# Weight sums of the down projection started during gate and up, and row scale and offset spread over its units

## Chip, cores and metric

One NeuronCore of one Trainium2 chip runs the whole program. The metric is the device time of one execution in microseconds, the median over the runs shown. All times below are of the kernel before the change.

## What is computed

The reference is a decoder trunk of two layers over 512 positions of width 1024, in float32:

```python
for l in range(DEPTH):                                   # DEPTH = 2
    proj = x @ w_in[l]
    ...
    mix = jnp.concatenate([o_a, o_b], axis=-1) @ w_out[l]
    x = layer_norm(ALPHA * x + mix, ln1_g[l], ln1_b[l])
    ffn = (jax.nn.silu(x @ w_ffn_gate[l]) * (x @ w_ffn_up[l])) @ w_ffn_down[l]
    x = layer_norm(ALPHA * x + ffn, ln2_g[l], ln2_b[l])
```

`o_a` is a gated linear recurrence and `o_b` sparse attention with three branches; the change does not edit them. D_FF is 2816, that is 22 blocks of 128 columns for each of gate and up, and 22 blocks of rows for the down projection. `layer_norm` subtracts the mean, divides by the deviation, multiplies by `g` and adds `b`.

## The kernel before

**Products.** Each float32 product is made of three matmuls (`mm3`, lines 80 to 86): an operand is split into a rounded part (`whi`, `hop`, `xh`, `th`), made by a cast on ACT, and the remainder (`wlo`, ...), made by a subtraction on DVE; the product is hi x hi, hi x lo and lo x hi.

**Gate and up.** `seven` (line 126) works through 20 units to a layer, gate and up in turn, each two blocks of 128 weight columns against the 512 positions in halves of 256. A unit makes seven products in place of eight, in Strassen's manner, so it needs sums of weight blocks. `stage` (lines 94 to 108) loads a unit's weights: SP issues the loads of `s1`, `s3`, the big `a` (128x1024) and `d`; POOL issues DMAs that add a second block into `s1` and `s3` (lines 104 and 105). DVE makes two more sums in `a` (lines 153 and 162). `split` (line 110) casts on ACT (line 116) and subtracts on DVE (line 117) into a ring of six places. Each unit finishes two of its products inside the next unit. A table of `hooks` lets other work be called at the head of a unit.

**Scale and offset of the rows.** The residual rows are four tiles of 128x1024. `norm_rest` (lines 751 to 759), called by the hook of unit 3, loads the parameters of the first norm (line 704, on POOL's queue) and issues for each tile one multiplication (line 756) and one addition (line 757) on DVE.

**Down projection.** It starts at line 1010. For four groups q, of two blocks of rows each, it again makes seven products of 2x2 blocks. The weight sums are made by DMAs: S1(q) = wd[1,2q] + wd[1,2q+1] is loaded by SP and added to by POOL in `raw_w` (lines 1034 to 1039; the load is line 1036, the add line 1038), S1(3) in a place of its own, `ws` (lines 1060 and 1061). `first` (line 1053) multiplies with S1 into the PSUM tiles Y and then has POOL add wd[0,2q] to it (line 1074); `third` (line 1081) multiplies with that sum into E and has POOL add wd[0,2q+1] (line 1087); `fourth` (line 1089) multiplies with the result into Z. `second` (line 1076) multiplies with the plain p11(q) into M. The list at lines 1092 to 1094 gives the order in which these are called, up to fourth(2). In the loop that follows, `raw_w` makes S3(q) = wd[0,2q] + wd[1,2q] in the same three places as the S1 sums (tag `f`), and loads p12 and p22; fourth(3) stands inside its first turn. The weights are split by `split` (lines 1016 to 1019) into three places for `whi` and three for `wlo`. In the trace Y is `ps_s`, E `ps_d`, Z `ps_t`, and M is `ps_h` and `ps_o`.

**Order.** Each engine works its instructions in order, and so do the DMA queues of SP and POOL: a DMA that waits holds those behind it. The order comes from a scheduler that goes by priorities (`high_priority`, with the offsets in the code) and by when it thinks operands and places come free. A tag with `bufs` is a set of places that tiles take in turn, and a tile waits until the last reader of its place is done.

Of the kernel before, what the change touches and what calls it, by code (L numbers as in the profile page):

```python
# [34 lines left out]
class Kern:  # L35
# [58 lines left out]
    def stage(self, sa, sb):  # L94

        nc = self.nc
        with self.tc.high_priority(offset=3000):
            self.turn += 1
            tag, bufs = ("wr", 2) if self.turn % 3 else ("pt", 2) if self.turn == 3 else ("f", 3)
            a = self.sb.tile([128, 1024], F32, name="wraw", tag=tag, bufs=bufs)  # L100
            s1, s3, d = (self.sb.tile([128, 512], F32, name=n, tag=t, bufs=2) for n, t in (("ws1", "st"), ("ws3", "pc"), ("wd", "wd")))
            nc.sync.dma_start(s1, sb[:, 512:])
            nc.sync.dma_start(s3, sa[:, :512])
            nc.gpsimd.dma_start(s1, sb[:, :512], accum_op=OP.add)
            nc.gpsimd.dma_start(s3, sb[:, :512], accum_op=OP.add)
            nc.sync.dma_start(a, sa)
            nc.sync.dma_start(d, sb[:, 512:])
        return a, s1, s3, d
# [17 lines left out]
    def seven(self, units, R, hooks):  # L126
# [13 lines left out]
        for n, unit in enumerate(units + [None]):  # L140
# [8 lines left out]
            if unit:  # L149
                self.prod(D, s1, R["T1"], True)  # L150
                y = copy("sy", D)
                with self.tc.high_priority(offset=3000):
                    nc.vector.tensor_tensor(a[:, :512], s1, a[:, :512], op=OP.add)
                self.prod(B, a[:, 512:], R["R21"], True)
                unit[2]("11", B, x)
# [606 lines left out]
    def layer(self, l):  # L762
# [242 lines left out]

        self.seven([(io[w][l, j], io[w][l, j + 1], f(j)) for j in range(2, NF, 2) for w, f in (("wg", gate), ("wu", up))], R,
                   {3: lambda: self.norm_rest(l, 0, rows, None)})

        QS = 4
# [4 lines left out]
        def split(dst, src):  # L1016
            with tc.high_priority(offset=3000):
                nc.scalar.copy(dst[0], src)  # L1018
                nc.vector.tensor_tensor(dst[1], src, dst[0].bitcast(F32), op=OP.subtract)  # L1019

        def places(k):
# [11 lines left out]

        def raw_w(src, plus=None, tag=("wr", 2)):
            t = self.sb.tile([128, 1024], F32, name="wraw", tag=tag[0], bufs=tag[1])
            nc.sync.dma_start(t, src)
            if plus is not None:
                nc.gpsimd.dma_start(t, plus, accum_op=OP.add)
            return t

        def dprod(acc, w, r, start, stop):
# [8 lines left out]
        half = [[(H[2 * q + e][:, :, b * 256:(b + 1) * 256]) for e in range(2) for b in range(2)] for q in range(QS)]  # L1050
        sums, ops = {}, {}

        def first(q):

            with tc.high_priority(offset=3000):
                if q < 3:
                    s = raw_w(wd[1, 2 * q], wd[1, 2 * q + 1], ("f", 3))
                else:
                    s = self.big("ws").rearrange("p a b -> p (a b)")[:, :1024]
                    nc.sync.dma_start(s, wd[1, 2 * q])  # L1060
                    nc.gpsimd.dma_start(s, wd[1, 2 * q + 1], accum_op=OP.add)
            r11, r12, _, r22 = half[q]
# [6 lines left out]
            with tc.high_priority(offset=3000):  # L1069
                nc.vector.scalar_tensor_tensor(r11, t1, -1.0, r22, op0=OP.mult, op1=OP.subtract)  # L1070
            sums[q] = s
            dprod(Y, split_w(s), o1, q == 0, q == QS - 1)
            with tc.high_priority(offset=3000):
                nc.gpsimd.dma_start(s, wd[0, 2 * q], accum_op=OP.add)

# [5 lines left out]
        def third(q):  # L1081
# [4 lines left out]
            with tc.high_priority(offset=3000):  # L1086
                nc.gpsimd.dma_start(sums[q], wd[0, 2 * q + 1], accum_op=OP.add)

        def fourth(q):
            dprod(Z, split_w(sums[q]), ops["22", q], q == 0, q == QS - 1)  # L1090

        for f, q in ((first, 0), (first, 1), (second, 0), (first, 2), (third, 0), (second, 1), (first, 3), (third, 1),
                     (fourth, 0), (second, 2), (third, 2), (fourth, 1), (second, 3), (third, 3), (fourth, 2)):
            f(q)
# [28 lines left out]
        for q in range(QS):  # L1123
# [3 lines left out]
            with tc.high_priority(offset=3000):  # L1127
                s3 = raw_w(wd[0, i], wd[1, i], ("f", 3))
                p12, p22 = raw_w(wd[0, i + 1]), raw_w(wd[1, i + 1])
# [6 lines left out]
            split(o4, r11)  # L1136
            dprod(Q, split_w(s3), o3, q == 0, end)
            dprod(M, split_w(p12), o21, False, False)
            if q == 0:
                fourth(QS - 1)  # L1140
            dprod(N, split_w(p22), o4, q == 0, end)
            if q == 0:
# [149 lines left out]
```

## Time and profile before

| what | value |
|---|---|
| median of three runs | 1347.09 us (1346.76, 1347.09, 1351.79) |
| profiled execution | 1353.65 us |
| its span, first to last instruction | 1351.9 us |
| mean granted clock of TensorE | 0.989 of full speed |
| PE, PEld busy | 97%, 89% |
| DVE, ACT, POOL busy | 75%, 55%, 14% |
| read from HBM, written | 180.76 MB, 7.10 MB |

PE stands for TensorE's matmuls, PEld for its weight loads, DVE for VectorE, ACT for ScalarE, POOL for GpSimd, SP for SyncE, which issues loads. A bracket behind a row gives how long the engine stood idle before the instruction and whose result ended that. A clock of 1.00 is 2.4 GHz. Layer 0's gate and up units run from about 350 to 560 us and its down projection to about 675; layer 1's from about 1020 to 1230 and from there to the end.

### The profile page before, as it was taken

The numbers are of one execution on the slowest core, as the hardware profiler recorded it, in microseconds if no ns is written. First come the engines' busy times: TensorE is split into PE (matmuls) and PEld (weight loads), VectorE is DVE, ScalarE is ACT, GpSimd is POOL, SyncE is SP. The second block draws the span as 40 slices with busy tenths as digits, with TensorE's granted clock in tenths as the row PEclk, the third lists the DMA queues.
The fourth block names the chain that finished last, engine by engine and source line by source line (L and its number), as shares of the span: only waits on it lengthen the run. The fifth ranks groups of instructions, "written<-read, shape, count | busy, mean of one in ns | idle before, by whom it ended". The sixth has DMA issues, their size and how long they took to land.

```text
span 1351.9 us, 23468 instructions
## 1 busy us (share of the span) xinstructions
PE 1311.2 (97%) x8853; PEld 1200.4 (89%) x8853; DVE 1012.4 (75%) x2021; ACT 749.6 (55%) x1495; POOL 192.5 (14%) x275
## 2 busy tenths in 40 slices
PE   8999999999999999999999999999999999999997
PEld 6988999789999999877899989987899999997776
DVE  4755798866887778967667668988559877788767
ACT  5254777844655555645452558777256555556530
POOL 1140111111011121110011100111010111111102
PEclk9999999999999999999999999999999999999999
DMA  7253212252467778586433221132515777866852
GB/s 236 79 164 102 79 56 74 84 161 76 149 167 185 189 189 197 136 223 174 152 140 116 73 92 63 63 102 71 166 29 179 178 184 180 215 158 150 213 196 79
DMA packets 67682, 186.54 MB, mean 138 GB/s; under 512 B 8175, under 2 KB 8351, under 8 KB 67056
## 3 DMA queue, kind: packets, MB, share of 16 engines
q1 hardware_dynamic: 44640, 124.73, 27.9%
q0 software_dynamic: 21920, 58.47, 21.2%
q10 hardware_dynamic: 1008, 1.84, 0.4%
q8 instruction: 69, 1.13, 0.3%
q14 instruction: 45, 0.37, 0.1%
HBM read 180.76 MB, written 7.10 MB: 139 GB/s over the span
## 4 chain that ended last, share of the span: by engine, by line
PE 59%; DVE 5%; DMA 5%; ACT 2%; issue 2%; POOL 0%; POOLq 0%; DVEq 0%; ACTq 0%
PE ps_d L83 10%; PE ps_d L82 10%; PE ps_d L84 10%; PE ps_t L84 3%; PE ps_t L82 3%; PE ps_t L83 3%; DMA wraw<-in_wd 3%; PE ps_s L82 2%; PE ps_s L83 2%; PE ps_s L84 2%; DMA ws<-in_wd 1%; PE ps_t L647 1%; DVE wlo L1019 1%; DVE hop L1019 1%; PE ps_h L390 1%
## 5 line engine op out<-in xcount | busy, mean ns | idle before, releaser
L116 ACT CAST whi<-wraw 128x512 fp32r<-128x512 f32 x160 | 98.6, 620 | 123.1 <-PE ps_d L83 93.3
L82 PE MATMUL ps_d<-xh,whi 128*128 128x256 f32 (+1 forms) x424 | 141.9, 338 | 2.0 <-ACT gates L497 1.2
L84 PE MATMUL ps_d<-xh,wlo 128*128 128x256 f32 (+1 forms) x424 | 142.6, 337 | 0.0
L83 PE MATMUL ps_d<-xl,whi 128*128 128x256 f32 (+1 forms) x424 | 141.7, 335 | 0.6 <-DVE mv L712 0.6
L117 DVE TENSOR_TENSOR wlo<-wraw,whi 128x512 fp32r<-128x512 f32 x160 | 108.9, 687 | 44.5 <-ACT whi L116 42.1
L84 PE MATMUL ps_d<-th,wlo 128*128 128x256 f32 x480 | 133.7, 284 | 2.4 <-DVE wlo L117 2.4
L83 PE MATMUL ps_d<-tl,whi 128*128 128x256 f32 x480 | 134.9, 283 | 0.0
L82 PE MATMUL ps_d<-th,whi 128*128 128x256 f32 x480 | 133.9, 283 | 0.1
L76 ACT CAST whi<-wraw 128x1024 fp32r<-128x1024 f32 (+1 forms) x68 | 70.7, 1040 | 97.0 <-PE ps_d L84 19.8
L77 DVE TENSOR_TENSOR wlo<-wraw,whi 128x1024 fp32r<-128x1024 f32 (+1 forms) x68 | 82.4, 1211 | 51.9 <-ACT whi L76 51.5
L84 PEld LDWEIGHTS ps_d<-th,wlo 128*128 128x128 f32 x480 | 91.2, 192 | 3.0 <-DVE wlo L117 3.0
L83 PEld LDWEIGHTS ps_d<-tl,whi 128*128 128x128 f32 x480 | 92.1, 192 | 0.1
L82 PEld LDWEIGHTS ps_d<-th,whi 128*128 128x128 f32 x480 | 91.4, 192 | 0.9 <-ACT su L136 0.5
L82 PEld LDWEIGHTS ps_d<-xh,whi 128*128 128x128 f32 x424 | 81.4, 193 | 9.2 <-ACT gates L497 1.3
L1019 DVE TENSOR_TENSOR wlo<-wraw,whi 128x1024 fp32r<-128x1024 f32 x50 | 60.6, 1219 | 38.3 <-ACT whi L1018 38.3
L83 PEld LDWEIGHTS ps_d<-xl,whi 128*128 128x128 f32 x424 | 81.9, 193 | 7.6 <-DVE mv L712 1.2
L84 PEld LDWEIGHTS ps_d<-xh,wlo 128*128 128x128 f32 x424 | 81.8, 193 | 7.5 <-DVE wlo L77 0.5
L83 PE MATMUL ps_d<-wlo,xh 128*128 128x256 f32 (+1 forms) x304 | 88.3, 291 | 0.0
L82 PE MATMUL ps_d<-whi,xh 128*128 128x256 f32 (+1 forms) x304 | 88.0, 291 | 0.0
L1018 ACT CAST whi<-wraw 128x1024 fp32r<-128x1024 f32 x50 | 52.3, 1051 | 64.1 <-DMA wraw<-in_wd 38.9
L84 PE MATMUL ps_d<-whi,xl 128*128 128x256 f32 (+1 forms) x304 | 87.8, 290 | 0.0
L608 ACT ACTIVATE e<-e,mn 128x128 f32<-128x128 f32 (+3 forms) x128 | 71.8, 564 | 22.1 <-DVE mn L606 21.7
(460 smaller groups left out, 4182.1 us busy)
## 6 DMA issues: line engine op xcount, KB each, us to landing
wraw<-in_wd SPq DMA_DIRECT2D x50, 512.0 KB, 4.2
wraw<-in_wf SPq DMA_DIRECT2D x31, 512.0 KB, 3.2
wraw<-in_wd POOLq DMA_DIRECT2D x26, 512.0 KB, 6.7
wraw<-in_wg SPq DMA_DIRECT2D x24, 512.0 KB, 3.9
wraw<-in_wu SPq DMA_DIRECT2D x24, 512.0 KB, 4.6
ws<-in_wg SPq DMA_DIRECT2D x40, 256.0 KB, 3.7
ws<-in_wg POOLq DMA_DIRECT2D x40, 256.0 KB, 4.7
ws<-in_wu SPq DMA_DIRECT2D x40, 256.0 KB, 3.6
```

The source lines that it names most:

```text
L76: nc.scalar.copy(h, raw[:, i:i + n])
L77: nc.vector.tensor_tensor(o, raw[:, i:i + n], h.bitcast(F32), op=OP.subtract)
L82: first = t.matmul(out, ah, bh, start=start, stop=False, **kw)
L83: t.matmul(out, ah, bl, start=False, stop=False, **kw)
L84: t.matmul(out, al, bh, start=False, stop=stop, **kw)
L116: nc.scalar.copy(h, raw)
L117: nc.vector.tensor_tensor(o, raw, h.bitcast(F32), op=OP.subtract)
L390: nc.tensor.matmul(p2[:, i], S[:, blk(i)], kq(128 * (i + 2), [[2 * w, n], [256 + w, 2], [1, w]]), start=True, stop=True)
L608: nc.scalar.activation(e, e, AF.Exp, bias=mn, scale=-1.0, accum_out=sm)
L647: nc.tensor.transpose(p[:, c:c + 128], E[qt][:, j * 128:(j + 1) * 128], self.ident)
L1018: nc.scalar.copy(dst[0], src)
L1019: nc.vector.tensor_tensor(dst[1], src, dst[0].bitcast(F32), op=OP.subtract)
```

## The change

Four things are edited.

- In `stage` the big `a` always takes one of two places (`wr`; unit 3 one of `pt`), where every third unit took one of the three places `f`. `self.tail` keeps the unit's last load, last add and the DVE sum, and `after` orders an instruction behind another one on the same engine or queue without a semaphore.
- S1(q) is loaded by the hooks of units 10, 12, 14 and 16 (`begin`) and added to by those of 11, 13, 15 and 17 (`go_on`), behind the unit's last load and last add. The sums of `first` and `third` go through `add_w`, which keeps POOL's adds in the order in which they are called.
- S3(q) gets places of its own, halves of a large tile `ws3`; `begin3` issues its load and add: (0) after third(1), (1) after third(2), (2) and (3) in the loop's first two turns.
- `norm_rest` is replaced by `rest`: the parameters are loaded at unit 2, one of the eight row operations stands in each of units 3 to 9 and the eighth in unit 11, behind the DVE sum of line 153.

```diff
--- before.py
+++ after.py
...
             self.turn += 1
-            tag, bufs = ("wr", 2) if self.turn % 3 else ("pt", 2) if self.turn == 3 else ("f", 3)
-            a = self.sb.tile([128, 1024], F32, name="wraw", tag=tag, bufs=bufs)
+            tag = "pt" if self.turn == 3 else "wr"
+            a = self.sb.tile([128, 1024], F32, name="wraw", tag=tag, bufs=2)
...
-            nc.gpsimd.dma_start(s3, sb[:, :512], accum_op=OP.add)
+            add = nc.gpsimd.dma_start(s3, sb[:, :512], accum_op=OP.add)
             nc.sync.dma_start(a, sa)
-            nc.sync.dma_start(d, sb[:, 512:])
+            self.tail = [nc.sync.dma_start(d, sb[:, 512:]), add, None]
...
                 with self.tc.high_priority(offset=3000):
-                    nc.vector.tensor_tensor(a[:, :512], s1, a[:, :512], op=OP.add)
+                    self.tail[2] = nc.vector.tensor_tensor(a[:, :512], s1, a[:, :512], op=OP.add)
...
+    def after(self, a, b):
+
+        self.tc.add_manual_dep(a.ins, b.ins.name, mybir.DependencyInfo(
+            mybir.DependencyClass.NoSync, mybir.DependencyReason.DATA), reason="queue order")
...
-        self.seven([(io[w][l, j], io[w][l, j + 1], f(j)) for j in range(2, NF, 2) for w, f in (("wg", gate), ("wu", up))], R,
-                   {3: lambda: self.norm_rest(l, 0, rows, None)})
...
+        def add_w(t, src):
+
+            d = nc.gpsimd.dma_start(t, src, accum_op=OP.add)
+            self.after(d, self.tail[1])
+            self.tail[1] = d
+
+        def halves(name):
+            b = self.big(name).rearrange("p a b -> p (a b)")
+            return [b[:, :1024], b[:, 1024:]]
+
+        sums = {}
+
+        def begin(q):
+            sums[q] = self.sb.tile([128, 1024], F32, name="wsum", tag="f", bufs=3) if q < 3 else halves("ws")[0]
+            self.after(nc.sync.dma_start(sums[q], wd[1, 2 * q]), self.tail[0])
+
+        def go_on(q):
+            add_w(sums[q], wd[1, 2 * q + 1])
+
+        lnps = []
+
+        def rest(i):
+            r, c = rows[i // 2], i % 2 * 1024
+            self.after(nc.vector.tensor_tensor(r, r, lnps[0][:, c:c + 1024], op=OP.add if i % 2 else OP.mult), self.tail[2])
+
+        hooks = {10 + 2 * q + e: lambda q=q, f=f: f(q) for q in range(QS) for e, f in enumerate((begin, go_on))}
+        hooks[2] = lambda: lnps.append(self.ln_params(l, 0))
+        for i in range(2 * NT):
+            hooks[i + 3 if i < 7 else 11] = lambda h=hooks.get(i + 3 if i < 7 else 11, lambda: None), i=i: (h(), rest(i))
+        self.seven([(io[w][l, j], io[w][l, j + 1], f(j)) for j in range(2, NF, 2) for w, f in (("wg", gate), ("wu", up))], R, hooks)
...
         def first(q):
 
-            with tc.high_priority(offset=3000):
-                if q < 3:
-                    s = raw_w(wd[1, 2 * q], wd[1, 2 * q + 1], ("f", 3))
-                else:
-                    s = self.big("ws").rearrange("p a b -> p (a b)")[:, :1024]
-                    nc.sync.dma_start(s, wd[1, 2 * q])
-                    nc.gpsimd.dma_start(s, wd[1, 2 * q + 1], accum_op=OP.add)
...
-            dprod(Y, split_w(s), o1, q == 0, q == QS - 1)
+            dprod(Y, split_w(sums[q]), o1, q == 0, q == QS - 1)
             with tc.high_priority(offset=3000):
-                nc.gpsimd.dma_start(s, wd[0, 2 * q], accum_op=OP.add)
+                add_w(sums[q], wd[0, 2 * q])
...
+        def begin3(q):
+            if q % 2 == 0:
+                s3s.extend(halves("ws3"))
+            with tc.high_priority(offset=3000):
+                nc.sync.dma_start(s3s[q], wd[0, 2 * q])
+                add_w(s3s[q], wd[1, 2 * q])
+
         for f, q in ((first, 0), (first, 1), (second, 0), (first, 2), (third, 0), (second, 1), (first, 3), (third, 1),
-                     (fourth, 0), (second, 2), (third, 2), (fourth, 1), (second, 3), (third, 3), (fourth, 2)):
+                     (begin3, 0), (fourth, 0), (second, 2), (third, 2), (begin3, 1), (fourth, 1), (second, 3), (third, 3),
+                     (fourth, 2)):
...
-                s3 = raw_w(wd[0, i], wd[1, i], ("f", 3))
...
-            dprod(Q, split_w(s3), o3, q == 0, end)
+            dprod(Q, split_w(s3s[q]), o3, q == 0, end)
...
+            if q < QS - 2:
+                begin3(q + 2)
```

The scheduler then puts other things in another order too. On DVE, in the first units of layer 0 (`r` is a row tile, `lnp` the parameters, `h_at` a hidden tile), there stood before

```order
L756 TENSOR_TENSOR r_2790<-r_2790,lnp_4124 128x1024 x2
L756 TENSOR_TENSOR r_2791<-r_2791,lnp_4124 128x1024 x2
L162 TENSOR_TENSOR wraw_3871<-wraw_3871 128x512
L117 TENSOR_TENSOR wlo_3773<-wd_3779,whi_3772 128x512
L978 TENSOR_TENSOR h_at_3836<-ps_t_3788,su_3852 128x256
L757 TENSOR_TENSOR r_2790<-r_2790,lnp_4124 128x1024
L117 TENSOR_TENSOR wlo_3775<-wraw_3871,whi_3774 128x512
L998 TENSOR_TENSOR up_3947<-ps_s_3882,sx_3898 128x256
L757 TENSOR_TENSOR r_2790<-r_2790,lnp_4124 128x1024
L117 TENSOR_TENSOR wlo_3773<-ws1_3998,whi_3772 128x512
L978 TENSOR_TENSOR h_at_3836<-ps_d_3786,sy_3819 128x256
L757 TENSOR_TENSOR r_2791<-r_2791,lnp_4124 128x1024
```

and now stands

```order
L153 TENSOR_TENSOR wraw_4003<-ws1_4004,wraw_4003 128x512
L1052 TENSOR_TENSOR r_2790<-r_2790,lnp_4001 128x1024
L117 TENSOR_TENSOR wlo_3779<-wraw_4003,whi_3778 128x512
L117 TENSOR_TENSOR wlo_3779<-wd_3878,whi_3778 128x512
L1003 TENSOR_TENSOR up_3951<-ps_t_3887,su_3982 128x256
L117 TENSOR_TENSOR wlo_3777<-wraw_4003,whi_3776 128x512
L1005 TENSOR_TENSOR h_at_3840<-up_3951,h_at_3840 128x512
L162 TENSOR_TENSOR wraw_4003<-wraw_4003 128x512
L117 TENSOR_TENSOR wlo_3777<-ws3_4005,whi_3776 128x512
L117 TENSOR_TENSOR wlo_3775<-wraw_4131,whi_3774 128x512
L153 TENSOR_TENSOR wraw_4131<-ws1_4132,wraw_4131 128x512
L1052 TENSOR_TENSOR r_2790<-r_2790,lnp_4001 128x1024
```

The multiplications and additions on the rows stood together at units 3 and 4; now one stands in each unit, the same eight operations in all.

On POOL's queue, from the end of layer 0's gate and up (`wraw` 6328, 6356, 6402 and `ws` 6470 hold S1(0) to S1(3), then `wraw` 6658, 6747 S3(0) and S3(1); `strip` and `cstrip` are loads for the attention), there stood before

```order
L1061 DMA ws_6470<-in_wd 128x1024
L1074 DMA wraw_6356<-in_wd 128x1024
L1074 DMA wraw_6402<-in_wd 128x1024
L323 DMA strip_8320<-Z_626 128x512
L1087 DMA wraw_6328<-in_wd 128x1024
L1074 DMA ws_6470<-in_wd 128x1024
L1087 DMA wraw_6356<-in_wd 128x1024
L1038 DMA wraw_6658<-in_wd 128x1024
L1087 DMA wraw_6402<-in_wd 128x1024
L1038 DMA wraw_6747<-in_wd 128x1024
L1087 DMA ws_6470<-in_wd 128x1024
```

and now stands, with `wsum` 5022, 5279, 5535 and `ws` 5791 for S1(0) to S1(3) and `ws3` for S3

```order
L1031 DMA wsum_5535<-in_wd 128x1024
L1031 DMA wsum_5022<-in_wd 128x1024
L1031 DMA ws_5791<-in_wd 128x1024
L1031 DMA wsum_5279<-in_wd 128x1024
L1031 DMA ws3_6520<-in_wd 128x1024
L1031 DMA wsum_5535<-in_wd 128x1024
L1031 DMA ws3_6520<-in_wd 128x1024
L1031 DMA ws_5791<-in_wd 128x1024
L1031 DMA ws3_6725<-in_wd 128x1024 x2
```

The add into S1(3) is gone from here (it stands among the units), the adds into S3(0) and S3(1) still stand among those that follow `third`, and the add after third(3) directly follows that into S3(1).

On PE, at the end of the gate and up units of layer 0 (`whi` 6386 and 6454 are p11(0) and p11(1), 6413 is S1(2), read by Y), there stood before

```order
L84 MATMUL ps_o_6321<-whi_6386,hop_6331 128x512
L83 MATMUL ps_s_6322<-wlo_6414,hop_6405 128x512
L84 MATMUL ps_s_6322<-whi_6413,hop_6405 128x512
L83 MATMUL ps_s_6323<-wlo_6414,hop_6405 128x512
L84 MATMUL ps_s_6323<-whi_6413,hop_6405 128x512
L82 MATMUL ps_s_6322<-whi_6413,hop_6405 128x512
L83 MATMUL ps_s_6322<-wlo_6414,hop_6405 128x512
L84 MATMUL ps_s_6322<-whi_6413,hop_6405 128x512
L82 MATMUL ps_s_6323<-whi_6413,hop_6405 128x512
L83 MATMUL ps_s_6323<-wlo_6414,hop_6405 128x512
L84 MATMUL ps_s_6323<-whi_6413,hop_6405 128x512
L82 MATMUL ps_h_6320<-whi_6454,hop_6359 128x512
```

and now stands, with 6392 and 6457 for p11(0) and p11(1), 6438 for third(0) and 6416 for S1(2)

```order
L82 MATMUL ps_o_6333<-whi_6392,hop_6340 128x512
L83 MATMUL ps_o_6333<-wlo_6393,hop_6340 128x512
L84 MATMUL ps_o_6333<-whi_6392,hop_6340 128x512
L82 MATMUL ps_h_6332<-whi_6457,hop_6365 128x512
L82 MATMUL ps_o_6333<-whi_6457,hop_6365 128x512
L82 MATMUL ps_d_6337<-whi_6438,hop_6433 128x512
L83 MATMUL ps_s_6334<-wlo_6417,hop_6408 128x512
L84 MATMUL ps_s_6334<-whi_6416,hop_6408 128x512
```

The first matmul with p11(1) now directly follows the last one with p11(0), where ten matmuls of Y stood between the two.

## Rows read from the trace of the kernel before

**Rows 1.** Busy time of each engine over the whole span, share, instructions.

```profile
PE 1311.2 (97%) x8853; PEld 1200.4 (89%) x8853; DVE 1012.4 (75%) x2021; ACT 749.6 (55%) x1495; POOL 192.5 (14%) x275
```

**Rows 2.** Windows: stretch, length, busy of PE, PEld, DVE, ACT, POOL, PE clock, DMA share, GB/s.

```profile
365.00:380.00 15.00, 12.67 (x101) 12.05 (x101) 15.00 (x24) 7.82 (x16) 0.85 (x1) 1.00 0.62 158
1035.00:1050.00 15.00, 12.27 (x95) 11.49 (x95) 15.00 (x25) 7.86 (x16) 0.84 (x1) 1.00 0.45 133
380.00:540.00 160.00, 160.00 (x1336) 160.00 (x1335) 124.46 (x223) 90.33 (x186) 30.16 (x35) 1.00 0.77 187
570.00:580.00 10.00, 8.95 (x39) 6.75 (x37) 7.30 (x9) 3.65 (x5) 2.57 (x3) 1.00 1.05 256
600.00:612.00 12.00, 9.49 (x37) 6.63 (x36) 9.76 (x14) 6.22 (x10) 1.71 (x2) 0.92 0.98 255
612.00:640.00 28.00, 28.00 (x122) 23.14 (x121) 20.46 (x25) 14.18 (x18) 0.00 (x0) 0.97 0.56 153
1240.00:1250.00 10.00, 8.42 (x36) 6.31 (x35) 6.79 (x9) 2.80 (x4) 2.56 (x3) 1.00 1.05 245
1250.00:1260.00 10.00, 9.33 (x34) 7.53 (x35) 5.50 (x6) 5.23 (x7) 1.74 (x2) 0.83 0.80 197
1270.00:1300.00 30.00, 28.82 (x127) 23.19 (x126) 25.46 (x32) 15.41 (x21) 2.29 (x3) 1.00 0.81 228
690.00:965.00 275.00, 268.93 (x1790) 244.26 (x1789) 208.88 (x528) 167.35 (x389) 35.61 (x56) 0.99 0.29 92
```

**Rows 3.** Waits of PE, 320 to 380 and 1020 to 1055: total, times, longest.

```profile
PE ps_t L82 <- ACT whi L116: 0.9, 1, 0.9
...
PE ps_d L84 <- DVE wlo L117: 1.6, 2, 1.2
```

**Rows 4.** Timeline of PE, layer 0's down projection: start, duration, engine, line, operation.

```profile
564.95 0.50 PE L82 MATMUL ps_d<-whi,hop 128*128 128x512 f32 x1 [0.33 <-ACT whi L1018]
...
580.34 0.73 PE L82 MATMUL ps_t<-whi,hop 128*128 128x512 f32 x2 [1.39 <-ACT whi L1018]
...
609.86 1.05 PE L82 MATMUL ps_t<-whi,hop 128*128 128x512 f32 x2 [2.02 <-ACT whi L1018]
```

**Rows 5.** Timeline of ACT in the same stretch.

```profile
579.24 1.04 ACT L1018 CAST whi<-wraw 128x1024 fp32r<-128x1024 f32 x1 [4.64 <-DMA wraw<-in_wd]
...
583.40 1.05 ACT L1018 CAST whi<-wraw 128x1024 fp32r<-128x1024 f32 x1 [1.63 <-PE ps_d L84]
...
591.10 1.05 ACT L1018 CAST whi<-ws 128x1024 fp32r<-128x1024 f32 x1 [1.15 <-PE ps_d L84]
...
608.76 1.04 ACT L1018 CAST whi<-ws 128x1024 fp32r<-128x1024 f32 x1 [5.78 <-DMA ws<-in_wd]
```

**Rows 6.** The chain that ended last: start, duration, what.

```profile
571.17 7.97 DMA wraw<-in_wd
...
598.63 10.04 DMA ws<-in_wd
```

**Rows 7.** Timeline of DVE in the first gate and up units.

```profile
361.05 4.62 DVE L756 TENSOR_TENSOR r<-r,lnp 128x1024 f32<-128x1024 f32 x4
...
367.13 1.21 DVE L757 TENSOR_TENSOR r<-r,lnp 128x1024 f32<-128x1024 f32 x1
```

**Rows 8.** DMA issues: destination, source, queue, count, KB each, median us to landing.

```profile
wraw<-in_wd SPq DMA_DIRECT2D x50, 512.0 KB, 4.2
...
wraw<-in_wd POOLq DMA_DIRECT2D x26, 512.0 KB, 6.7
wraw<-in_wg SPq DMA_DIRECT2D x24, 512.0 KB, 3.9
```

**Rows 9.** Timeline of POOL in layer 0's down projection.

```profile
598.09 0.85 POOL L1038 DMA_DIRECT2D wraw<-in_wd  x1 [10.09 <-DMA wraw<-in_wd]
598.63 1.20 POOL L1087 DMA_DIRECT2D ws<-in_wd  x1
```

**Rows 10.** Waits of SP's DMA queue over the whole span: total, times, longest.

```profile
SPq L106 <- DVE wlo L117: 88.3, 27, 8.1
```

More of the change, by code (lines that the diff above doesn't have):

```diff
@@ L1019, in split, with raw_w @@
                 nc.vector.tensor_tensor(dst[1], src, dst[0].bitcast(F32), op=OP.subtract)
+        def raw_w(src):
+            t = self.sb.tile([128, 1024], F32, name="wraw", tag="wr", bufs=2)
+            nc.sync.dma_start(t, src)
+            return t
+        def add_w(t, src):
[20 more added lines that the diff above has]
+        self.seven([(io[w][l, j], io[w][l, j + 1], f(j)) for j in range(2, NF, 2) for w, f in (("wg", gate), ("wu", up))], R, hooks)
         def places(k):
@@ L1032, in split_w @@
             return w
[L1034 to L1039, printed above, removed]
         def dprod(acc, w, r, start, stop):
@@ L1050, in layer @@
         half = [[(H[2 * q + e][:, :, b * 256:(b + 1) * 256]) for e in range(2) for b in range(2)] for q in range(QS)]
-        sums, ops = {}, {}
+        ops, s3s = {}, []
         def first(q):
-            with tc.high_priority(offset=3000):
-                if q < 3:
-                    s = raw_w(wd[1, 2 * q], wd[1, 2 * q + 1], ("f", 3))
-                else:
-                    s = self.big("ws").rearrange("p a b -> p (a b)")[:, :1024]
-                    nc.sync.dma_start(s, wd[1, 2 * q])
-                    nc.gpsimd.dma_start(s, wd[1, 2 * q + 1], accum_op=OP.add)
             r11, r12, _, r22 = half[q]
@@ L1070, in first @@
                 nc.vector.scalar_tensor_tensor(r11, t1, -1.0, r22, op0=OP.mult, op1=OP.subtract)
-            sums[q] = s
-            dprod(Y, split_w(s), o1, q == 0, q == QS - 1)
+            dprod(Y, split_w(sums[q]), o1, q == 0, q == QS - 1)
             with tc.high_priority(offset=3000):
-                nc.gpsimd.dma_start(s, wd[0, 2 * q], accum_op=OP.add)
+                add_w(sums[q], wd[0, 2 * q])
         def second(q):
@@ L1086, in third @@
             with tc.high_priority(offset=3000):
-                nc.gpsimd.dma_start(sums[q], wd[0, 2 * q + 1], accum_op=OP.add)
+                add_w(sums[q], wd[0, 2 * q + 1])
         def fourth(q):
             dprod(Z, split_w(sums[q]), ops["22", q], q == 0, q == QS - 1)
+        def begin3(q):
[4 more added lines that the diff above has]
+                add_w(s3s[q], wd[1, 2 * q])
         for f, q in ((first, 0), (first, 1), (second, 0), (first, 2), (third, 0), (second, 1), (first, 3), (third, 1),
-                     (fourth, 0), (second, 2), (third, 2), (fourth, 1), (second, 3), (third, 3), (fourth, 2)):
+                     (begin3, 0), (fourth, 0), (second, 2), (third, 2), (begin3, 1), (fourth, 1), (second, 3), (third, 3),
+                     (fourth, 2)):
             f(q)
```

## The prediction, made before the changed kernel ran

> **What bounds the kernel now.** I began with the busy time of each engine over the whole span. The reader is to see one engine far ahead of the rest: PE is busy in 1311.2 of 1351.9 us [rows 1], so all that can be won without removing matmuls is 40.7 us of PE idle time. The change removes no matmul, so the question is where that idle time lies. The windows answer it by stage [rows 2]. Inside gate and up PE has no gap at all (160.00 of 160.00 us, 1336 matmuls, so 0.1198 us each); there the work is PE's. It has gaps in the first units after the norm (365 to 380 us: 12.67 of 15.00; 1035 to 1050: 12.27 of 15.00), where DVE is busy for the whole 15.00, and at the start of the down projection (570 to 580: 8.95 of 10.00; 600 to 612: 9.49 of 12.00; 1240 to 1250: 8.42 of 10.00), where the DMA share is 0.98 to 1.05. Then I read what ended those gaps: after the norm PE waits for `whi` and `wlo` of the gate/up split [rows 3]; in the down projection its timeline [rows 4] waits for ACT's cast of a weight sum, ACT waits for the DMA that adds into it [rows 5], and the chain that ended last runs through the same DMAs [rows 6]. The median run is 1347.09 us; the profiled execution is 1353.65, 6.56 us (0.5%) longer. I work the sum on the profile and put the difference on the median. About 0.5%, some 6.7 us, is what a measurement of this kernel tells from no change: faster means under 1340.4 here, slower over 1353.8.
>
> **Part 1: scale and offset of the rows, one operation to a unit.** Before, the eight 128x1024 operations on the rows stand close together: four in a row on DVE, 4.62 us, then four of 1.21 us between single splits [rows 7]. That is 4.62 + 4 x 1.21 = 9.5 us of DVE in some 15 us in which DVE was full. After, one 1.21 us operation stands in each of seven units and one more later. A unit is 84 matmuls, 84 x 0.1198 = 10.06 us, and DVE is free in (160.00 - 124.46)/160.00 = 22% of a steady stretch, 2.2 us to a unit, so the operation fits. The gaps of both windows, 2.33 and 2.73 us, should go: **-5.1 us**. Bounds: 0 (the first units wait for their own operands anyway) and -5.1; if that cover is gone, one operation can delay one split by 1.21 us, which the six-place ring of splits lies ahead of (a product is 12 matmuls, 1.44 us). The parameter load of 1 MB moves from unit 3 to unit 2 on POOL's queue; it lies in a stretch without PE waits on DMA, cost nothing.
>
> **Part 2: third(0) to fourth(0), and a wait that the new order adds.** Before, the add into S1(0) after third(0) takes 7.97 us to land [rows 6], where the median of these adds is 6.7 and of the plain loads 4.2 [rows 8]; the cast follows at 579.24 [rows 5] and PE starts at 580.34 after 1.39 us idle [rows 4]. The windows around give 1.05 us of idle in layer 0, 1.58 in layer 1 [rows 2]. In layer 1 the clock is 0.83 after that gap, so of 10 us some 1.7 go too. Together 1.05 + 1.58 + 1.7 = 4.3 us. The order on PE, however, now lets the first matmul of M on p11(1) follow the last one on p11(0) directly, where ten matmuls of Y lay between. There are three places for `whi`, and the cast for p11(1) takes the place that this last matmul reads; such a cast waiting for PE is in the trace ("1.63 <-PE ps_d L84", [rows 5]). So PE must wait for a cast, 1.05 us [rows 5], and two handovers, some 0.07 us each way by the 579.24 + 1.04 to 580.34 of [rows 4, 5]: 1.2 us. The cast of third(0), now two matmuls ahead of its use instead of more, costs perhaps 0.65 us against the 0.33 seen [rows 4]. That is 1.85 us to a layer, 3.7 us. It stands ahead of fourth(0)'s wait: if the chain through the DMA is as long as before, PE waits less at fourth(0) by what it waited here and the new waits cost nothing; if the chain shortens, the old wait goes and the new ones are paid. The first case is worth 0, the second -4.3 + 3.7 = **-0.6 us**, which I take; bounds -4.3 (the new waits are hidden) and +3.7 (fourth(0)'s wait stays whole besides).
>
> Whether the chain shortens depends on the S3 loads. S1(3), a load and an add of 512 KB, leaves this stretch; the loads of S3(0) and S3(1), 512 KB each, enter it some microseconds ahead of the add in question, when the last product of the gate/up units has freed their places. On SP the loads of p11(2), p11(3) and p12(0) stand behind them; those need places that come free no sooner, so that wait costs nothing by itself. The same holds for S3(2) and S3(3), which wait until second(2) is through PE, with p22(0) behind them. The DMA share there is 1.05 already [rows 2]. The Trainium skill ("DMA: Bandwidth & Descriptors", Issuing engines are not separate DMA queues) says that transfers issued by SP, ACT and POOL run on the same 16 DMA engines and interleave; by that rule the two loads on SP's queue stretch the add on POOL's as much as if they shared a queue, and the whole sum below would be that of my first rival. The trace agrees so far that these adds are slowest where the share is highest.
>
> **Part 3: the add after third(3) no longer stands behind S3's.** Before, POOL's queue holds the add into S3(1) at 598.09, after waiting 10.09 us for S3(1)'s own load, and the add after third(3) goes out only behind it, at 598.63 [rows 9]. It takes 10.04 us [rows 6], the cast starts at 608.76 [rows 5], PE at 609.86 after 2.02 us idle [rows 4]. Third(3)'s own data was there at 592.15 (the cast of `ws` at 591.10 took 1.05, [rows 5]) plus the DVE split, some 1.2 us like the row operations of the same shape [rows 7]: 593.4, so 5 us earlier. After, S3(1)'s load goes out at that earlier point, not when an S1 place comes free, and its add waits for nothing late. PE's need is at 609.86 - 2.02 = 607.84; even 10.04 us from 593.4 lands at 603.4, with the cast 604.5. So the wait goes: 12.00 - 9.49 = 2.51 us, and the low clock that follows it, (1 - 0.92) x 12 = 0.96 and (1 - 0.97) x 28 = 0.84 [rows 2]. In layer 1 the same add and S3(2) and S3(3) cost the idle time of 1270 to 1300, 30.00 - 28.82 = 1.18 [rows 2]. Together 2.51 + 0.96 + 0.84 + 1.18 = **-5.5 us**; bounds 0 (another wait of that size takes its place) and -5.5. Late next are the casts that wait for a free `whi` place, each under half a us.
>
> **Part 4: what moves in gate and up.** S1(0) to S1(2) were loaded and added there before as well, by the order of POOL's queue; only S1(3) is new there. Each S1 load and add now stands behind the last load and add of its unit, on SP and POOL; the stretch has a DMA share of 0.77 [rows 2] and PE no gap. The big `a` of every third unit had a place in another ring before; now all turn in two places: a lead of one unit, 10.06 us, less the 3.9 us of a landing [rows 8]. Cost 0; bounds 0 and the second rival's price.
>
> **Part 5: the layer-1 mixer** is ordered a little differently without having been edited. PE idles 275.00 - 268.93 = 6.07 us there [rows 2], so it can win at most that, and lose as much by the same kind of waits. I take 0, +-4.
>
> **The sum:** -5.1 - 0.6 - 5.5 = -11.2 us. The profiled execution would go from 1353.65 to 1342.4; the median to **1336 us**.
>
> **Rivals.** First, **the S3 loads crowd the stretch** and the add after third(0) lands later. The two loads are 1.05 MB; at the 256 GB/s of 570 to 580 [rows 2] that is 4.1 us, which S1(3)'s bytes, gone from there, had taken too, but earlier; I price the shift at half, 2 us to each layer, and the new waits of 3.7 are paid besides: -5.1 + 4 + 3.7 - 5.5 = -2.9, 1344. For it: a share of 1.05 with no room. Against: no byte is added. Second, **the slower one: `a` comes late.** Its load can go out only when DVE has read the unit before last; SP already waits 88.3 us in 27 pieces, up to 8.1, for that [rows 10]. It decides if a landing takes longer than the 10.06 us of a unit less the cast, about 9 us, as the 10.04 of [rows 6] does in a crowd. Then each of some 36 units (20 to a layer, less the first two) loses about half a microsecond: +18, and 1336 + 18 = 1354, or more where the clock falls too. Against: landings of gate weights are 3.9 [rows 8] at a share of 0.77. Third, **the change does not do what it says**: S1 was early already, and the add after third(3) still stands directly behind S3(1)'s in POOL's queue. If S3(1)'s load is late, only part 1 stays: 1342.
>
> **How the numbers follow.** The forecast gets 0.52 (with its bounds 1330 to 1340.5), the crowd 0.20 (1340 to 1347), the late `a` 0.08 (1352 and up), no effect but part 1's 0.15 (1340 to 1345), the rest 0.05 is the mixer's order, either way. Faster by over 0.5%: nearly all of the forecast and a third of the crowd and of the third rival, 0.62. Same: 0.30. Slower: 0.08. The range 1329 to 1346 leaves out the late `a` and the ends of the crowd.
>
> **What would show it.** In 365 to 380 and its counterpart PE busy over 14.5 of 15, no group of four row operations: part 1. A wait of about 1.2 us on PE at the first matmul of M with p11(1): part 2; fourth(0)'s wait under 0.5. No wait over 1 us at fourth(3), and POOL's add after third(3) issued before 595: part 3. PE full in gate and up, with SP's waits for `a` no longer than a unit: part 4. Wrong if PE's idle time there is unchanged, or if gaps appear inside gate and up.

## The result, and the profile after

| | before | after |
|---|---|---|
| median of all its runs | 1349.86 us (6 runs) | 1340.53 us (1337.26 to 1344.32, 6 runs) |
| profiled execution, its span | 1353.65, 1351.9 us | 1337.49, 1335.7 us |
| granted clock over the span | 0.989 | 0.996 |

The ratio is 0.993, 95% interval 0.9906 to 0.9955: the kernel became faster, by 9.3 us where 11.2 were forecast. (The forecast of 1336 us stood on the three runs of before, median 1347.09; with three more it is 1349.86.) The windows of the changed kernel's profile, same columns as [rows 2], taken where its stages now lie:

```profile
365.00:380.00 15.00, 15.00 (x128) 15.00 (x127) 13.75 (x24) 7.96 (x16) 1.70 (x2) 1.00 0.71 176
380.00:540.00 160.00, 160.00 (x1336) 160.00 (x1335) 128.91 (x224) 90.01 (x184) 29.30 (x34) 1.00 0.81 205
...
556.00:570.00 14.00, 11.61 (x54) 8.90 (x53) 14.00 (x23) 8.12 (x12) 3.19 (x5) 1.00 0.82 214
570.00:580.00 10.00, 10.00 (x44) 7.94 (x43) 8.46 (x11) 4.70 (x6) 2.57 (x3) 1.00 1.02 212
580.00:600.00 20.00, 20.00 (x90) 16.57 (x89) 14.05 (x17) 10.71 (x14) 4.26 (x5) 1.00 1.04 252
600.00:612.00 12.00, 12.00 (x54) 9.94 (x53) 12.00 (x15) 9.88 (x13) 0.00 (x0) 1.00 0.54 137
...
1035.00:1050.00 15.00, 15.00 (x127) 15.00 (x126) 13.42 (x24) 9.13 (x18) 2.18 (x3) 1.00 0.67 172
...
1226.00:1240.00 14.00, 13.85 (x54) 11.32 (x55) 12.22 (x16) 5.25 (x6) 4.28 (x5) 0.88 0.89 176
```

PE is full in both first stretches, in gate and up as before, and from 570 to 612, where [rows 2] had gaps. One stretch is worse: 556 to 570, with 2.39 us idle. PE's timeline there (answers to [rows 4]):

```profile
561.30 0.50 PE L82 MATMUL ps_d<-whi,hop 128*128 128x512 f32 x1 [0.55 <-ACT whi L1021]
...
565.25 0.50 PE L82 MATMUL ps_h<-whi,hop 128*128 128x512 f32 x1 [1.14 <-ACT whi L1021]
...
566.92 0.50 PE L83 MATMUL ps_s<-wlo,hop 128*128 128x512 f32 x1 [0.70 <-DVE wlo L1022]
```

The first is the wait for the cast of third(0), the second that for the cast of p11(1), both named in the prediction; the third, for the remainder of S1(2), was not forecast. POOL no longer holds the add after third(3) behind one into S3 that waits for its load: it goes out at 590.60, as soon as DVE has split (598.63 in [rows 9]). The first row is the add into S3(1), the second the add after third(3):

```profile
583.72 0.89 POOL L1031 DMA_DIRECT2D ws<-in_wd  x1
590.60 0.85 POOL L1031 DMA_DIRECT2D ws<-in_wd  x1 [5.99 <-DVE wlo L1022]
```

**Pauses by stage.** For all runs I added up PE's pauses over 0.3 us, each the distance of two matmul starts in the timeline less the matmul's own time (0.12 us for 256 columns, 0.23 for 512). "Down" begins with its first matmul; the mixer columns hold the rest up to the gate/up units.

| run | ratio to before, interval | mixer 0 | gate/up 0 | down 0 | mixer 1 | gate/up 1 | down 1 |
|---|---|---|---|---|---|---|---|
| before | 1 | 14.1 | 2.8 | 5.4 | 9.7 | 3.1 | 4.4 |
| the change | 0.993 (0.9906 to 0.9955) | 14.9 | 0 | 2.9 | 12.9 | 0 | 2.9 |
| e1_rows_together | 0.9966 (0.9944 to 0.9989) | 13.6 | 2.8 | 2.5 | 12.1 | 2.7 | 2.5 |
| e2_s3_shared | 0.9999 (0.9977 to 1.0021) | 16.2 | 0 | 6.9 | 9.4 | 0 | 8.3 |
| e3_s1_late | 0.9927 (0.9895 to 0.9959) | 14.9 | 0.6 | 2.8 | 11.7 | 0 | 2.1 |
| e4_y_between | 0.9933 (0.9912 to 0.9955) | 13.9 | 0 | 3.8 | 11.5 | 0 | 3.5 |
| e5_s3_prep_late | 0.9888 (0.986 to 0.9916) | 14.6 | 0 | 2.9 | 10.9 | 0 | 0.7 |
| e7_s1_late_prep_late | 0.9961 (0.9941 to 0.9982) | 15.7 | 0.4 | 4.6 | 13.9 | 0.6 | 3.3 |
| e8_rows_alone | 0.9955 (0.9933 to 0.9977) | 13.5 | 0 | 5.0 | 12.2 | 0 | 3.8 |
| e9_s3_alone | 1.0107 (1.0077 to 1.0137) | 15.5 | 9.1 | 2.8 | 11.6 | 9.5 | 4.0 |
| e10_rows_on_before | 0.9948 (0.9927 to 0.997) | 15.1 | 0 | 3.2 | 12.0 | 0 | 3.7 |
| e11_s3_on_before | 1.0084 (1.006 to 1.0108) | 13.9 | 2.8 | 9.4 | 11.7 | 3.6 | 8.8 |
| e12_both_on_before | 1.0049 (1.0025 to 1.0073) | 15.1 | 0 | 9.5 | 11.3 | 0 | 10.6 |
| e13_prep_in_two | 0.9884 (0.9854 to 0.9913) | 13.6 | 0 | 1.4 | 11.9 | 0 | 0 |

### The profile page after: what moved, and what is told of

Same layout as the page of the kernel before. It is cut to its first block, busy times and chain, and to the rows that moved or that the text cites. A ratio compares the mean times of both kernels' runs of the same rounds, so it can differ in the third digit from the quotient of the medians.

```text
span 1335.7 us, 23468 instructions
## 1 busy us (share of the span) xinstructions
PE 1300.6 (97%) x8853; PEld 1195.6 (90%) x8853; DVE 1012.7 (76%) x2021; ACT 751.8 (56%) x1495; POOL 191.4 (14%) x275
## 4 chain that ended last, share of the span: by engine, by line
PE 87%; DVE 6%; ACT 3%; DMA 2%; issue 2%; POOL 0%; POOLq 0%; DVEq 0%; ACTq 0%
PE ps_d L82 15%; PE ps_d L83 15%; PE ps_d L84 15%; PE ps_t L82 4%; PE ps_t L83 4%; PE ps_t L84 4%; PE ps_s L83 4%; PE ps_s L84 3%; PE ps_s L82 3%; PE ps_t L652 2%; PE ps_h L395 2%; PE ps_o L663 1%; PE ps_o L84 1%; PE ps_o L83 1%; PE ps_o L662 1%
## 5 line engine op out<-in xcount | busy, mean ns | idle before, releaser
L611 DVE CUSTOM_DVE_ANT_0 e<-ps_s,strip 128x128 f32<-128x128 f32 (+3 forms) x128 | 59.1, 485 | 15.2 <-PE ps_s L626 12.1
L116 ACT CAST whi<-ws 128x512 fp32r<-128x512 f32 x80 | 49.5, 619 | 25.4 <-ACT sy L136 10.4
```

The costliest lines, as they stand in the source:

```text
L116: nc.scalar.copy(h, raw)
L611: nc.vector.tensor_tensor_reduce(out=e, in0=pa, in1=st[:, 512 - pa.shape[-1]:], scale=1.0, scalar=3e38, op0=OP.add, op1=OP.min, accum_out=mn)
```

## The experiments

**Undoing the spread rows.** `hooks[2]` and the loop over `rest` give way to one line:

```diff
-        hooks[2] = lambda: lnps.append(self.ln_params(l, 0))
-        for i in range(2 * NT):
-            hooks[i + 3 if i < 7 else 11] = lambda h=hooks.get(i + 3 if i < 7 else 11, lambda: None), i=i: (h(), rest(i))
+        hooks[3] = lambda: self.norm_rest(l, 0, rows, None)
```

> The changed kernel with the eight row operations put back together at unit 3. Theory A (the burst holds up the splits on DVE): the PE gaps in the first gate/up units come back, 2.3 to 3.4 us in each layer, some 5.5 us in all, while the rest of the change keeps its gain: no wait over 1 us at fourth(0) and fourth(3); time 1341 to 1346 against 1340.5 of the change, since the order on PE at p11(1) also goes back to that of before (ten Y matmuls in between). Rival B (the gaps came from the place or order of the loads of those units): the burst stands there and PE has no gap over 0.5 us in 360 to 380; 1337 to 1341.

1344.79 us. The same three waits as before the change came back (waits of PE, 355 to 385 us):

```profile
PE ps_t L82 <- ACT whi L116: 0.9, 1, 0.9
PE ps_d L84 <- DVE wlo L117: 0.8, 1, 0.8
PE ps_t L84 <- DVE wlo L117: 0.6, 1, 0.6
```

Theory A holds: 2.8 and 2.7 us of pauses in the first units, 4.3 us in time (the intervals of the two ratios just overlap; the rows alone on the kernel before, below, are clear of 1). PE's order at p11(1) is that of before again, and its waits at the start of the down projection are others: 1.23 us for a hidden tile and 0.90 for the remainder of p11(0).

**Undoing S3's places.**

```diff
-                nc.sync.dma_start(s3s[q], wd[0, 2 * q])
-                add_w(s3s[q], wd[1, 2 * q])
+                pass
...
+                s3 = self.sb.tile([128, 1024], F32, name="wraw", tag="f", bufs=3)
+                nc.sync.dma_start(s3, wd[0, i])
+                nc.gpsimd.dma_start(s3, wd[1, i], accum_op=OP.add)
```

> The changed kernel with S3 back in the three places of the S1 sums, its load and add called in the loop. Theory A (the add after third(3) stood behind the add into S3(1)): POOL issues the add after third(3) at the same moment as one into S3, fourth(3) waits 1 to 2.2 us in layer 0 and the Y matmuls after it 0.4 to 0.8, about 4 us for both layers with a stretch of low clock behind each wait over 2 us; 1343 to 1347. Rival B (the earlier S1 loads alone removed those waits): no wait over 0.5 us at fourth(3); 1340 to 1342.

1349.43 us, over the range of both theories: all of the change's gain is gone. Line 1159 is S3's add, line 1031 one of the others; POOL's and PE's timelines:

```profile
600.13 0.85 POOL L1159 DMA_DIRECT2D wraw<-in_wd  x1 [9.96 <-DMA wraw<-in_wd]
600.67 1.18 POOL L1031 DMA_DIRECT2D ws<-in_wd  x1
```

```profile
600.22 0.73 PE L82 MATMUL ps_t<-whi,hop 128*128 128x512 f32 x2 [1.29 <-ACT whi L1021]
...
611.48 0.73 PE L82 MATMUL ps_t<-whi,hop 128*128 128x512 f32 x2 [0.42 <-ACT whi L1021]
...
612.95 0.73 PE L82 MATMUL ps_s<-whi,hop 128*128 128x512 f32 x2 [0.74 <-ACT whi L1021]
```

The add after third(3) again goes out in the shadow of one into S3, and the one after third(2) too, so that PE waits at two of the `fourth` products (`ps_t`), and at a product of the loop behind them (`ps_s`).

**S1 not pinned to units.** `begin` and `go_on` are called in `first` at high priority, as the loads were before, without the edges to the unit's last load and add.

```diff
-        hooks = {10 + 2 * q + e: lambda q=q, f=f: f(q) for q in range(QS) for e, f in enumerate((begin, go_on))}
+        hooks = {}
...
+            with tc.high_priority(offset=3000):
+                begin(q)
+                go_on(q)
```

> The changed kernel with the S1 loads and adds called in the down projection as before (no hooks at units 10 to 17), S3 in its own places. Theory A (S1(0) to S1(2) came during gate and up anyway, only S1(3) moved): no change that can be told, 1339 to 1343, PE waits at the start of the down projection as in the change or as before in order, but none over 1.5 us; the DMA share at 556 to 570 stays under 1. Rival B (the early S1 loads are what frees the stretch): the add after third(0) takes over 7.5 us to land and fourth(0) waits 1.4 to 2.4 us again; 1344 to 1348.

1338.83 us: by the time theory A, but the waits are those of rival B: the add after third(0) takes 10.76 us and fourth(0) waits 1.58. "Late" is only where the call stands. With the `f` places free, the scheduler sent S1(0) to S1(2) earlier, not later (348 us); only S1(3) came back into the down projection. PE's order at p11(1) is that of before again too. So the waits ahead of fourth(0) are gone (0.40 us is left), fourth(0) waits instead, and the sum is about the same (2.8 and 2.1 us against 2.9 and 2.9). That early calls make no difference here is two differences that cancel.

**PE's order alone.** `dprod` returns its matmuls, and:

```diff
+            if q == 1:
+                for x in m:
+                    self.after(x, ys[2][3])
```

> The changed kernel with one order edge on PE: the matmuls with p11(1) stand behind those of first(2). Theory A (the new PE waits, 1.1 us for the cast of p11(1) and 0.7 for the remainder of S1(2), 2.2 us with handovers, come from the place that the cast needs): the 1.1 us wait goes in both layers and no other grows; 1336 to 1338. Rival B (DVE is full there, 14.00 of 14.00 us, and the remainder of S1(2) is late anyway): PE now waits 2 to 3 us for that remainder at the first matmuls of Y, and the time stays at 1340 to 1342.

1341.01 us: rival B. With Y between, no wait for the cast is left, but PE stands still for DVE:

```profile
564.56 0.50 PE L82 MATMUL ps_d<-whi,hop 128*128 128x512 f32 x1 [1.07 <-DVE h_e L1008]
566.29 0.77 PE L83 MATMUL ps_s<-wlo,hop 128*128 128x512 f32 x1 [1.23 <-DVE wlo L1022]
```

DVE is full from 556 to 570, 14.00 of 14.00 us, as in the changed kernel. What it does just ahead of that split stands in the chain that ended last of the changed kernel:

```profile
561.37 0.42 DVE h_e L1008
561.79 0.60 DVE h_qs L1161
562.39 0.60 DVE h_at L1166
563.00 1.27 DVE hop L1022 x3
...
565.65 1.23 DVE wlo L1022
566.92 0.50 PE ps_s L83
```

Lines 1161 and 1166 are differences of hidden tiles for the products with S3, forty microseconds and more ahead of their use. A full DVE alone is not the cause: it was as full in the kernel before, with two such differences (there lines 1130 and 1135) in the same stretch, and PE waited only once at the start of that down projection, 0.49 us. They stood earlier there, 2.7 and 7.2 us behind the first matmul of the down projection where the changed kernel has them at 10.4 and 11.0. Window (columns of [rows 2]) and DVE's timeline of the kernel before:

```profile
556.00:570.00 14.00, 13.67 (x70) 11.12 (x69) 14.00 (x23) 10.48 (x16) 4.57 (x6) 1.00 0.90 198
```

```profile
556.50 0.68 DVE L1130 TENSOR_TENSOR h_qs<-h_qs 128x512 f32<-128x512 f32 x1
...
561.04 0.68 DVE L1135 SCALAR_TENSOR_TENSOR h_at<-h_at 128x512 f32<-128x512 f32 x1
```

**Those differences held back**, first all behind the DVE half of fourth(0)'s split, kept as `ops["lo"]`, with S1 pinned and not, then in two steps:

```diff
-                nc.vector.tensor_tensor(r12, r22, r12, op=OP.subtract)
+                self.after(nc.vector.tensor_tensor(r12, r22, r12, op=OP.subtract), ops["lo"])
...
-                nc.vector.scalar_tensor_tensor(r11, r11, -1.0, r21, op0=OP.mult, op1=OP.subtract)
+                self.after(nc.vector.scalar_tensor_tensor(r11, r11, -1.0, r21, op0=OP.mult, op1=OP.subtract), ops["lo"])
```

> The changed kernel with DVE's eight differences of hidden tiles for the S3 products (two to each q) held back behind the split of fourth(0)'s weights; the order on PE follows. Theory A (DVE's backlog at the end of gate and up sets the new waits, 2.4 us more than before in each layer): with some 1.8 us of DVE work out of the way, the waits of 0.72, 1.30 and 0.87 us shrink to 1 us in all or less, in both layers; 1336 to 1338. Rival B (the chain of adds through the DMA is next): those waits go, but fourth(0) waits 1 to 2 us; 1339 to 1341.

> The same with S1 called late. Theory A (calling S1 early is worth nothing by itself): within 2 us of the run with S1 early, 1336 to 1340, fourth(0) waiting as there. Rival B (with DVE relieved the early S1(3) matters, since its load and add crowd the add after third(0)): fourth(0) waits 1.5 us or more longer than in the run with S1 early; 1340 to 1343.

1336.9 and 1346.6 us. The first bears out theory A: no wait over 0.3 us at the start of the down projection. One moved: eight held-back operations now stand on DVE between fourth(0)'s split and that of p11(2), and PE waits for the latter.

```profile
588.02 0.50 PE L83 MATMUL ps_h<-wlo,hop 128*128 128x512 f32 x1 [1.39 <-DVE wlo L1022]
```

This run does not separate DVE from PE, since the scheduler put PE's order back too: the ten matmuls of Y (`ps_s`) again stand between p11(0) and p11(1), DVE being just as full (14.00 of 14.00 us). PE's timeline of this run, the last matmul with p11(0), the first of the ten, the first with p11(1):

```profile
568.03 0.39 PE L84 MATMUL ps_o<-whi,hop 128*128 128x512 f32 x1
568.34 0.50 PE L83 MATMUL ps_s<-wlo,hop 128*128 128x512 f32 x1
...
570.74 0.39 PE L82 MATMUL ps_h<-whi,hop 128*128 128x512 f32 x1
```

The second is slower than either theory allowed. fourth(0), without a pause over 0.3 us in the first, now pauses 0.89 us, and 0.69 more for its remainder, in layer 0, and 0.69 in layer 1: rival B's sign, in layer 0 only. Pauses of 4.3 us more in both down projections (4.6 + 3.3 against 2.9 + 0.7) and 3 us more in mixer 1 go with S1's loads left to the scheduler; what ties the mixer's to them I leave open.

> The changed kernel with DVE's differences for S3 held back in two steps, those of q = 0 behind fourth(0)'s split and the others behind fourth(1)'s. Where all were held behind fourth(0)'s, they stood ahead of the split of p11(2) and PE waited 1.56 us for it in layer 0. Theory A (DVE's order alone sets that wait): it falls under 0.3 us, the rest stays, 1334 to 1336.5. Rival B (the differences now come late for S3(0) and the later products): a new wait of 1 us or more at the first matmuls with S3, 1336 to 1339.

In both edits above `ops["lo"]` is then `ops["lo", min(q, 1)]`. 1332.67 us, the lowest median here and under both ranges; by its ratio it is not told from the first of these runs (0.9884 and 0.9888). DVE holds only the two operations of q = 0 ahead of p11(2)'s split, the others behind fourth(1)'s. Theory A: that wait is gone, none came at the products with S3. In layer 0 two waits of about half a microsecond are left, for a remainder and for the cast of the weights that follow; layer 1's down projection has no wait at all:

```profile
PE ps_h L82 <- ACT wx L76: 0.6, 1, 0.6
PE ps_t L83 <- DVE wlo L1022: 0.5, 1, 0.5
```

**Each part alone.** Two runs started from the changed kernel, with S1 unpinned, and S3's places or the rows undone besides.

> The row operations spread, but S1 called late and S3 in the shared places: of the change little but the spreading (and the order of POOL's first and third adds) is left. Theory A (the spreading is worth the idle time of the first units by itself): 5 to 6 us under the kernel before, 1344 to 1346. Rival B (it is given back: PE comes earlier to the down projection, whose sums come no sooner, and waits there): no gap in the first units, but the waits at fourth(0), fourth(2) and fourth(3) grow by 4 to 6 us in all over those of before; 1348 to 1351.

> S3 in its own places, but the row operations together and S1 called late. Theory A (S3's places are worth the waits at fourth(3) and the low clock behind them, 5.5 us, whatever the rows do): 1343 to 1346, gaps of 2.3 to 3.4 us in the first units of each layer, no wait over 1 us at fourth(3), fourth(0)'s wait as before or shorter. Rival B (the two parts only work together): 1347 to 1350.

1345.08 us, theory A; and 1365.87 us, which neither theory foresaw. The loss is not in the down projection. The unpinned S1 adds went out at 355 to 359 us, on POOL's queue ahead of the load of the norm's parameters, and the row operations, in one burst, held DVE until it had landed:

```profile
371.25 4.63 DVE L761 TENSOR_TENSOR r<-r,lnp 128x1024 f32<-128x1024 f32 x4 [7.29 <-DMA lnp<-in_ln]
```

So this run does not tell what S3's places are worth. The next three start from the kernel before, with S1 and the big `a` as there: `rest` and its hooks alone; `begin3` and the `ws3` places alone, its adds and the others left to the scheduler; and both.

```diff
+        hooks = {2: lambda: lnps.append(self.ln_params(l, 0))}
+        for i in range(2 * NT):
+            hooks[i + 3 if i < 7 else 11] = lambda i=i: rest(i)
...
+                nc.sync.dma_start(s3s[q], wd[0, 2 * q])
+                nc.gpsimd.dma_start(s3s[q], wd[1, 2 * q], accum_op=OP.add)
...
-                s3 = raw_w(wd[0, i], wd[1, i], ("f", 3))
```

> The kernel before with one edit: the row operations spread over units 3 to 9 and 11. Theory A (the spreading is worth the idle time of the first units by itself): no gap over 0.6 us in the first units and 5 to 6 us less than the kernel before. Rival B (it is given back at the sums of the down projection, which come no sooner): the waits at fourth(0) and fourth(3) grow by 2 to 3 us in each layer, and the time is 0 to 2 us under that of before.

> The kernel before with one edit: S3 in its own places, begun where the changed kernel begins it, POOL's adds left to the scheduler's order. Theory A (S3's places are worth the waits at fourth(3) and the low clock behind them): no wait over 0.6 us at fourth(3), 4 to 6 us less than before, the gaps in the first units unchanged. Rival B (what the add after third(3) no longer waits for is waited for elsewhere, since POOL's queue now holds S3's adds ahead of those after first(2) and third(0)): fourth(0) waits 1 us or more longer than before, and the time is 0 to 2 us under that of before.

> The kernel before with both edits, without S1's loads pinned to units, without POOL's order of the adds, the third place for the big a as before. Theory A (the whole change is these two): 8 to 11 us less than before, as the changed kernel. Rival B (the pinned loads and adds carry part of it): at most 6 us less than before, with waits over 1.5 us left at fourth(0).

The rows alone: 1344.24 us, theory A, 0.5% by themselves. S3's places alone: 1360.74 us, slower than before, and both together, 1357.38, slower than before too, which no theory had foreseen. For S3's places it is rival B's reason, far beyond its numbers: POOL sends S3's adds (line 1059) ahead of those after first(2) and third(0) (lines 1082, 1095), and PE waits 6.55 us at fourth(0). POOL's timeline, the chain and PE's timeline of the run with S3's places alone:

```profile
565.61 1.81 POOL L1059 DMA_DIRECT2D ws<-in_wd  x2 [2.84 <-DMA ws<-in_wd]
567.12 1.18 POOL L1082 DMA_DIRECT2D wraw<-in_wd  x1
...
568.95 0.85 POOL L1095 DMA_DIRECT2D wraw<-in_wd  x1
```

```profile
568.95 15.71 DMA wraw<-in_wd
```

```profile
585.86 1.22 PE L82 MATMUL ps_t<-whi,hop 128*128 128x512 f32 x2 [6.55 <-ACT whi L1018]
```

The run with S1 unpinned (0.9927) is its counterpart in this stretch: S1(3)'s add goes out at 561.00 against 561.05 there, the add after third(0) at 568.92 against 568.95, but POOL's order is kept and S3's adds go out only at 576.04 and later. Its chain and its fourth(0):

```profile
568.92 10.76 DMA wsum<-in_wd
```

```profile
580.87 0.73 PE L82 MATMUL ps_t<-whi,hop 128*128 128x512 f32 x2 [1.58 <-ACT whi L1021]
```

Issued at the same moment, the add takes 5 us less, and PE's wait is shorter by the same 5 us. In both runs the adds landed in the order of issue, from the one at 561.0 on about 3 us apart (2.5 to 3.9); the one after third(0) is fourth in that row and lands at 579.67, or sixth, behind the two into S3, and lands at 584.66.

The run with S1 unpinned also has the rows spread, loads S1(0) to S1(2) earlier and keeps the big `a` out of the `f` places. The rows are not the reason: with both parts on the kernel before they are spread as well, and the same add in its chain took

```profile
570.80 16.01 DMA wraw<-in_wd
```

The other two are argued away only by the stretch itself: in the 20 us ahead of the wait SP's and POOL's issues are the same but for the place of S3's adds, and the add after first(2), which stands behind them, goes out 1.75 us later. No run takes POOL's order edges alone out of the changed kernel.

## Why the prediction was right, and where it was not

**The total** was right in size (-11.2 forecast, -9.3 measured, inside the range), and the shares it rested on are only partly so. Some of that is luck: of the -11.2, -7.7 were idle time of PE and -3.5 low clock. By the table the pauses of gate, up and the down projections fell by 9.9 us, more than forecast, those of the two mixers grew by 4.0, and what the clock gave is not known (below).

**Part 1** was right: -5.1 forecast, the pauses of the first units (2.8 and 3.1 us) gone, 4.3 us when undone and 7.0 (1351.23 - 1344.24) when done alone; nothing came in their place inside gate and up.

**Part 2** failed in the step that sized the new waits, "PE must wait for a cast" and "1.85 us to a layer", and in its term for the clock. The two waits I named came, 1.30 and 0.72 us by the distance of starts, but a third came with them, 0.87 us for the remainder of S1(2): 2.89 us to a layer. I had put the cause in the places for `whi`. With p11(1) held behind Y by hand the cast's wait went, but PE waited no less, for DVE; with DVE's early differences held back, and PE's order back too, all three went. So the waits hang on what DVE does ahead of those splits, not on the place alone; whether DVE's order would do without PE's was not run, and a full DVE by itself does not make them (the kernel before). What the part added up came nearly so in idle time: 1.55 + 2.41 us at fourth(0) went, 2 x (2.89 - 0.49) came (0.49 was there before), +0.8 where 3.7 - 2.63 = +1.1 stood. But the two do not trade with each other: with the differences held back neither is there. The -1.7 for the clock did not come: in layer 1 the stretch of low clock only moved, to behind the new wait (0.88 from 1226 to 1240) from behind the old one.

**Part 3** was right in the waits: 2.19 + 0.82 + 0.36 and 0.77 + 0.73 us, 4.9 in all, are gone, with the low clock at 610; undoing the places cost 8.9 us. What it left out is why they are safe to move. Places of their own are not enough, as the two runs on the kernel before show, where they made the kernel slower; where POOL's adds also keep the order of need, they are worth the gain. I had named the order edges in the change and given them no term.

**Part 4** was right: no gap in gate and up. S1's early calls, taken out alone, cost nothing (0.9927 without, 0.993 with), but that was two effects that cancel; with the differences held back they are worth 0.7% (0.9961 without, 0.9888 with). The second rival, late `a`, left no trace.

**Part 5:** the pauses of mixer 1 grew from 9.7 to 12.9 us, and by 1 to 4 in all other variants but one; inside the 4 allowed.

**The first rival** is the one to learn from. It did not happen in the changed kernel: S3's loads do go out in that stretch (560.20), but the add after third(0), issued at 568.30 and 1227.53, took 7.7 and 6.6 us in the two layers, where it had 7.97 [rows 6] and 8.8. The profile's row for the one in layer 0, the time to landing last:

```profile
wsum<-in_wd POOLq DMA_DIRECT2D x1, 512.0 KB, 7.7
```

The crowd is real all the same. With S1(3) still in that stretch (S1 unpinned) the add took 10.76; with S3's adds ahead of it as well 15.71, and fourth(0) waited 5.2 and 3.8 us more than in the kernel before, against the 2 us that I priced. SP sends S3's loads at the same time in these two runs (559.68 and 559.70), so the last 5 us belong to the adds on POOL's queue, of which the rival did not think. "No byte is added" was no argument: all these kernels read the same bytes. The Trainium skill ("DMA: Bandwidth & Descriptors", Issuing engines are not separate DMA queues) says that transfers issued by SP, ACT or POOL run on the same 16 DMA engines and interleave. In these runs the share of the engines is full (1.05), but none separates SP's loads from POOL's adds; among POOL's adds the order of issue decided whose wait it became.

**What rests on the clock.** Windows of 5 us over the two profiles up to 1330 us, each with the missing share of its clock, add up to 11.9 us before and 3.4 after: seven short stretches against two, five of the seven in places that the change does not edit. The runs of the changed kernel differ in their clock as well: 1335.5 us of span at 0.996, 1342.5 at 0.992. So the 16.2 us between the two profiles are about 6 us of pauses (39.5 against 33.6 by the table) and 8.5 of clock; how much of the 9.3 between the medians is clock was not separated.

## What to carry to other kernels

Where several transfers share an in-order queue and the DMA engines are full, giving one of them its own buffer lets it start earlier and so stand ahead of the one that is needed first: keep the queue in the order of need, and count an order edge as a term of the sum. A wait that names one resource (a place for a cast) can stand on top of another (an engine that is late); test it by moving work off that engine, not only by reordering the one that waits. Work with a far-off use that the scheduler pulls forward is the first to hold back.

## What was not expected of the hardware

More transfers in flight did not show as a higher share but as time to land: from 570 to 580 the share was 1.05 to 1.07 in the kernel before, with S1 unpinned and with S3's places alone, and the add after third(0), of 512 KB, took 7.97, 10.76 or 15.71 us by what had been issued ahead of it. And a PE pause was followed by a stretch at the lower of the two clock levels (2.4 and 1.2 GHz) in some places and not in others: the changed kernel has the same three waits in both layers, 2.89 us, and the clock fell only in layer 1 (0.88 from 1226 to 1240, 1.00 from 556 to 580). Each such stretch (a window of 5 us at some 0.66, 0.34 x 5) cost about 1.7 us, as much as most of the waits that this change is about.
